# Second half of the modulation sums: from VectorE to ScalarE and GpSimd

## The chip, the cores and the metric

The kernel runs on one core of a Trainium2 chip. The core has TensorE (PE) for matrix products, VectorE (DVE) and ScalarE (ACT) for work on rows of elements, GpSimd (POOL) for the same without access to PSUM, and SyncE (SP), whose queue issues the loads here. The metric is device time in microseconds of one execution, as the median over runs.

## The reference

Two transformer blocks on 256 tokens of 1024 features, in float32. The first has a modulation vector, two attentions with gates, and a mixture of 32 experts of which each token takes 4; the second has three attentions, gates and a feed-forward part. What bears on the change is the modulation:

```
mod_x = (silu(c) @ w_ada + b_ada)[:, None, :]          # 1024 -> 6 x 1024
sh_a, sc_a, g_a, sh_m, sc_m, g_m = split(mod_x, 6)
...
x = x + g_a * merge(attention(modulate(rmsnorm(x), sh_a, sc_a)))
x = x + g_m * moe(modulate(rmsnorm(x), sh_m, sc_m))
```

The first two parts are needed before the first projection. The other four (`g_a`, `sh_m`, `sc_m`, `g_m`) are needed at the end of the attention and in the expert part.

## The kernel before, in words

The kernel goes through three stages: a dense one (projections of the first block, its two attentions, gates, output), the experts, and the second block. All weights pass through a ring of tiles of 128x2048 floats (1 MB each) that SP's queue loads in the order of a list, `specs`; a tile's slot is given back by `free(key)`, and the next load waits for a slot. Each weight of a dense projection is split into two parts that TensorE multiplies in turn: ACT copies it rounded (`wh`, L316), DVE subtracts (`wl`, L319). Split tiles rotate over a few buffers.

The first two parts of the modulation come from TensorE (`ada_first`). The other four come in two groups (g = 1 and 2) of 2048 columns each. For a group the list holds eight `ada` tiles (j = 0 to 7), 128 rows of `w_ada` each, spread among the weights of the projections. `ada_one`, called when certain weight quarters are done, takes the next such tile and multiplies it by the column `ada_s[:, j, 0:1]` (one value for each partition). For each half of 1024 columns it adds the product to an accumulator, `ga_b` (first half) or `gm_b` (second half), at L626; for j = 0 it writes the product alone, at L624. After j = 7 matmuls with a matrix of ones add the accumulators over the partitions (L633), and transposes bring the result into `mod` and `abp`.

Between the projections the kernel works through a list of small steps (`bg`), among them the attentions. `attend_a` has 16 units: scores on PE, their maximum on DVE (L831, L832), the exponential on ACT (L834), the reciprocal on DVE (L835), the scale of the probabilities on POOL (L856), transposes on PE (L866), copies on DVE or ACT, and the product with the values (L878). `attend_b` has 8 units of two maps each: the second map is scaled on POOL (L917), DVE combines it with the first (L918), then come transposes (L926), copies (L928) and products (L936).

The program is written in the order of the code, and a planner sets the order of each engine's instructions, with estimates of their durations and with semaphores for all dependencies; on the chip each engine runs its own list strictly in that order.

Of the kernel before, what the change touches and what calls it, by code (L numbers as in the profile page):

```python
# [13 lines left out]
AF = mybir.ActivationFunctionType  # L14
OP = mybir.AluOpType
# [3 lines left out]
D = 1024  # L19
# [56 lines left out]
def build(tc, I, out):  # L76
    nc = tc.nc
    V, S, G, PE = nc.vector, nc.scalar, nc.gpsimd, nc.tensor
# [12 lines left out]
    def bank(which="a", dt=F32, shape=(128, 512)):  # L91
        return psp.tile(list(shape), dt, name="bank_" + which, tag="bank")
# [172 lines left out]
    def free(key):  # L265
        live.pop(key)
        in_extra.discard(key)
        fill()
# [162 lines left out]
    gm_b = keep.tile([128, D], F32, name="gm_b")  # L431
# [84 lines left out]
    def body():  # L516
# [10 lines left out]
        ga_b = p1.tile([128, D], F32, name="ga_b")  # L527
# [31 lines left out]
        ada_s = p1.tile([128, 8, 32], F32, name="ada_s")  # L559
# [10 lines left out]
        for tt in range(2):  # L570
            scaled = G.tensor_scalar(out=xn[:, tt], in0=x_sb[:, tt], scalar1=rx[:, tt:tt + 1], scalar2=1.0,
                                     op0=OP.mult, op1=OP.mult)
# [43 lines left out]
        def ada_one():  # L616


            g, j = ada_queue.pop(0)
            w = live[("ada", g, j)]  # L620
            for c, acc in enumerate((ga_b, gm_b)):
                o = slice(1024 * c, 1024 * c + 1024)
                if j == 0:
                    V.tensor_scalar(out=acc, in0=w[:, o], scalar1=ada_s[:, j, 0:1], scalar2=None, op0=OP.mult)  # L624
                else:
                    V.scalar_tensor_tensor(out=acc, in0=w[:, o], scalar=ada_s[:, j, 0:1], in1=acc,  # L626
                                           op0=OP.mult, op1=OP.add)
            free(("ada", g, j))
            if j < 7:
                return  # L630
            ps = bank("b")
            for c in range(4):
                PE.matmul(ps[32 * c:32 * c + 32], one_row, (ga_b, gm_b)[c // 2][:, 512 * (c % 2):512 * (c % 2) + 512],  # L633
                          start=True, stop=True)
            mrow = p1.tile([128, 512], F32, name="mrow", tag="mrow")
            V.tensor_copy(mrow, ps)
            pt = bank("b", shape=(128, 4, 128))
            for i in range(4):
                PE.transpose(pt[:, i], mrow[:, 128 * i:128 * i + 128], ident)
            bias = cols[:, 48 + 16 * g:64 + 16 * g].rearrange("p (c i) -> p i c", c=4)  # L640
            V.tensor_tensor(mod[:, g], pt.rearrange("p i (c r) -> p i c r", r=32)[:, :, :, 0:2],
                            bias.unsqueeze(3).to_broadcast([128, 4, 4, 2]), op=OP.add)
            ps = bank("b", shape=(128, 2, 2, 128))
            for b in range(2):
                for e in range(2):
                    PE.transpose(ps[:, b, e], mrow[:, 256 * b + e:256 * b + 256:2], ident)
            v = ps.rearrange("p b e (c r) -> p c b e r", r=32)[:, (2, 0)[g - 1]:(4, 2)[g - 1], :, :, 0]
            for h in range(2):
                V.tensor_tensor(abp[:, 2 - g, h], v[:, h], cols_p[:, g - 1, h], op=OP.add)
            if g == 2:  # L650
                V.scalar_tensor_tensor(out=abp[:, 0], in0=abp[:, 0], scalar=1.0, in1=cols_p[:, 2], op0=OP.add,
                                       op1=OP.mult)
            if g == 1:
                grow = cg.rearrange("p k t d -> p (k t d)")
                add_row(grow, 0, mrow, 0)
                late["row"] = grow
            if g == 2:
                add_row(mrow, 2, mrow, 1)
                late["rows"] = mrow

        ada_step.append(ada_one)

        def add_row(dst, c0, mrow, k):
            brow = pp.tile([128, 512], F32, name="brow", tag="pexp1")
            for h in range(2):
                b0 = 32 * (c0 + h)
                f0 = 2048 + 3072 * k + 512 * h
                with tc.issue_after(split_last[0].ins):
                    nc.scalar.dma_start(out=brow[b0:b0 + 1], in_=I["b_ada"][:, f0:f0 + 512])
                V.tensor_tensor(dst[b0:b0 + 1], mrow[b0:b0 + 1], brow[b0:b0 + 1], op=OP.add)  # L670
# [314 lines left out]
        for tt in range(2):  # L985
            G.tensor_scalar(out=xc[:, tt], in0=xc[:, tt], scalar1=rc[:, tt:tt + 1], scalar2=1.0,
                            op0=OP.mult, op1=OP.mult)
# [74 lines left out]
        for k in range(2):  # L1062
            V.scalar_tensor_tensor(out=lj, in0=lams[:, 2 * k], scalar=1.0, in1=lams[:, 2 * k + 1],
                                   op0=OP.mult, op1=OP.mult, accum_out=lam[:, k:k + 1])
# [18 lines left out]
        while ada_queue:  # L1083
            ada_one()
# [27 lines left out]
        for h in range(2):  # L1112
# [3 lines left out]
            for q in range(4):  # L1116
# [5 lines left out]
                for m in range(4):  # L1122
                    for k in range(2):
                        i = 2 * (q % 2) + k
                        o = dst[m // 2][:, m % 2]
                        c = slice(128 * m, 128 * m + 128)
# [7 lines left out]
            for b in range(2):  # L1134
                j = 4 * h + 2 * b
# [8 lines left out]
                               op0=OP.add, op1=OP.mult)  # L1144
# [884 lines left out]
```

## Time and profile before

| | us |
|---|---|
| median of 3 runs | 1704.33 |
| lowest, highest | 1698.94, 1705.49 |
| profiled execution | 1698.37 |
| its span | 1696.6 |

In the profiled execution PE is busy for 1621.6 us of the span, DVE for 695.2, ACT for 466.0 and POOL for 81.8. Busy times are averages over stages with different limits, so they are read stage by stage: which engine or transfer has no gap there, and what the others wait for. A matmul's end is modelled, so a busy PE need not be PE at its peak. POOL's spans are rough.

### The profile page before, as it was taken

To read this page: it belongs to the slowest core of one execution; us is meant where nothing else is said; L and a number is where in the kernel's file an instruction comes from. 1 tells how busy PE (TensorE), PEld (TensorE's weight loads), DVE (VectorE), ACT (ScalarE), POOL (GpSimd) and SP (SyncE) were. 2 spreads that over 40 slices of the span, in tenths; PEclk is the share of its full clock that TensorE was granted. 3 is DMA by queue.
4 is the path that set the end of the run, shared out by engine and by line. 5 is a ranking of instruction groups with operands and counts; after the bars stand their busy time and mean duration, and the time that the engine had idled before them with its cause. 6 is when DMAs were issued, how large, how long until landed. Compare 5 with 4: busy or idle time off the path is not lost. (4 is left out here: it accounts for less than half of the span.)

```text
span 1696.6 us, 22129 instructions
## 1 busy us (share of the span) xinstructions
PE 1621.6 (96%) x9024; PEld 1012.3 (60%) x9024; DVE 695.2 (41%) x1348; ACT 466.0 (27%) x768; POOL 81.8 (5%) x112
## 2 busy tenths in 40 slices
PE   5999899999999999899999999999999999999997
PEld 3777797544434443354344334433388899989996
DVE  4898986311121111221211111111267556665555
ACT  3435564101000100110000001000256445454443
POOL 2102100000000000000000000000004101100001
PEclk9999999999999999999999999999999999999999
DMA  9643588999999999999999999999973433565540
GB/s 344 260 154 141 202 282 335 382 425 425 426 426 425 425 425 426 382 425 425 425 426 425 425 426 426 426 422 424 405 277 102 146 121 131 178 218 184 176 153 25
DMA packets 117035, 537.42 MB, mean 317 GB/s; under 512 B 11666, under 2 KB 13438, under 8 KB 66754
## 3 DMA queue, kind: packets, MB, share of 16 engines
q1 hardware_dynamic: 112144, 532.19, 78.4%
q10 hardware_dynamic: 4610, 3.52, 0.7%
q8 instruction: 72, 1.18, 0.3%
q0 software_dynamic: 176, 0.26, 0.1%
q14 instruction: 33, 0.27, 0.0%
HBM read 534.88 MB, written 1.05 MB: 316 GB/s over the span
## 5 line engine op out<-in xcount | busy, mean ns | idle before, releaser
L1381 PE MATMUL bank_a<-w,xg 128*64 128x512 f32 x2048 | 522.5, 599 | 2.2 <-DMA w<-in_w_up_dram 2.2
L1381 PEld LDWEIGHTS bank_a<-w,xg 128*64 128x64 f32 x2048 | 182.7, 137 | 280.9 <-issue 258.5
L319 DVE TENSOR_TENSOR wl<-w,wh 128x1024 fp32r<-128x1024 f32 (+1 forms) x193 | 236.2, 1228 | 153.0 <-ACT wh L316 145.1
L316 ACT ACTIVATE wh<-w 128x1024 fp32r<-128x1024 f32 (+1 forms) x193 | 202.1, 1049 | 220.1 <-PE bank_a L389 98.7
L1381 PE MATMUL bank_a<-w,at 128*64 128x512 f32 x960 | 228.4, 595 | 6.5 <-DVE e L1409 5.0
L390 PE MATMUL bank_a<-hi,wl 128*128 128x256 f32 x640 | 180.3, 283 | 1.0 <-DVE wl L319 1.0
L388 PE MATMUL bank_a<-hi,wh 128*128 128x256 f32 x616 | 176.3, 287 | 1.1 <-ACT hi L474 0.6
L389 PE MATMUL bank_a<-lo,wh 128*128 128x256 f32 x616 | 174.3, 283 | 0.2 <-DVE lo L475 0.2
L1381 PEld LDWEIGHTS bank_a<-w,at 128*64 128x64 f32 x960 | 83.5, 137 | 146.6 <-issue 102.9
L513 ACT ACTIVATE y<-bank_a,ws 128x512 fp32r<-128x512 f32 x32 | 22.0, 687 | 443.1 <-PE bank_a L1381 429.9
L390 PEld LDWEIGHTS bank_a<-hi,wl 128*128 128x128 f32 x640 | 122.3, 192 | 1.4 <-DVE wl L319 1.4
L388 PEld LDWEIGHTS bank_a<-hi,wh 128*128 128x128 f32 x616 | 117.8, 192 | 3.2 <-issue 0.9
L389 PEld LDWEIGHTS bank_a<-lo,wh 128*128 128x128 f32 x616 | 118.1, 192 | 0.9 <-DVE lo L475 0.6
L514 DVE SCALAR_TENSOR_TENSOR y<-bank_a,ws,y 128x512 fp32r<-128x512 f32 x32 | 24.0, 751 | 217.9 <-ACT y L513 216.2
L1409 DVE TENSOR_SCALAR e<-bank_a 128x512 f32<-128x512 f32 x32 | 22.1, 691 | 187.1 <-PE bank_a L1381 185.9
L1399 ACT ACTIVATE e<-gs 128x512 f32<-128x512 f32 x32 | 20.2, 630 | 236.7 <-DVE gs L1398 225.2
L1291 PEld LDWEIGHTS bank_a<-gr,x_sb 128*128 128x128 f32 x512 | 64.2, 196 | 23.0 <-issue 19.5
L1398 DVE TENSOR_SCALAR gs<-bank_a 128x512 f32<-128x512 f32 x32 | 22.0, 691 | 131.2 <-PE bank_a L1381 115.8
L1291 PE MATMUL bank_a<-gr,x_sb 128*128 128x128 f32 x512 | 69.3, 286 | 0.7 <-DVE gr L1274 0.7
L1296 DVE TENSOR_SCALAR xg<-bank_a,abp 128x128 f32<-128x128 f32 x64 | 21.9, 404 | 107.7 <-PE bank_a L1291 107.5
L1299 ACT ACTIVATE xg<-bank_a,abp 128x128 f32<-128x128 f32 x64 | 24.2, 455 | 121.8 <-PE bank_a L1291 121.7
L354 PE MATMUL bank_b<-wh,hh 128*128 128x512 f32 x128 | 49.9, 390 | 0.0
(453 smaller groups left out, 2198.4 us busy)
## 6 DMA issues: line engine op xcount, KB each, us to landing
w<-in_w_up_dram SPq DMA_DIRECT2D x144, 1024.0 KB
w<-in_w_down_dram SPq DMA_DIRECT2D x136, 1024.0 KB
w<-in_w_gate_dram SPq DMA_DIRECT2D x128, 1024.0 KB
w<-in_w_in_dram SPq DMA_DIRECT2D x45, 1024.0 KB
w<-in_w_ada_dram SPq DMA_DIRECT2D x16, 1024.0 KB
w<-in_w_ada_dram SPq DMA_DIRECT2D x16, 512.0 KB
w<-in_w_out_dram SPq DMA_DIRECT2D x8, 1024.0 KB
w<-in_w_down_dram SPq DMA_DIRECT2D x16, 512.0 KB
```

The source lines that it names most:

```text
L316: split_last[0] = S.activation(r32(wh[:, :n]), t[:, o:o + n], AF.Copy)
L319: V.tensor_tensor(r32(wl[:, :n]), t[:, o:o + n], wh[:, :n], op=OP.subtract)
L354: PE.matmul(o, r32(sh), r32(mh), start=first, stop=False)
L388: PE.matmul(o, r32(wh[:, k, c]), r32(hi[:, j]), start=j == 0 and m % 2 == 0, stop=False)
L389: PE.matmul(o, r32(wh[:, k, c]), r32(lo[:, j]), start=False, stop=False)
L390: PE.matmul(o, r32(wl[:, k, c]), r32(hi[:, j]), start=False, stop=j == 7 and m % 2 == 1)
L513: S.activation(r32(hi), src, AF.Copy, scale=scale)
L514: V.scalar_tensor_tensor(out=r32(lo), in0=src, scalar=scale, in1=hi, op0=OP.mult, op1=OP.subtract)
L1291: PE.matmul(ps[:, k], x_sb[:, tt, o:o + 255:2], d["gr"][:, tt].rearrange("p e s -> p (e s)"), start=tt == 0, stop=tt == 1)
L1299: S.activation(xg[:, j], ps[:, k], AF.Identity, bias=abp_[:, 1, j:j + 1], scale=abp_[:, 0, j:j + 1])
L1381: state["mm"] = PE.matmul(ps[h][64 * ab:64 * ab + 64], lhs(j, ab), w[ab][:, e, 512 * h:512 * h + 512], start=bias is None and j == 0, stop ...
L1409: V.tensor_scalar(out=u_, in0=ps[h], scalar1=7.0, scalar2=-7.0, op0=OP.min, op1=OP.max)
```

## The change

For the second half of the columns, ACT multiplies the half of the `ada` tile in place by the column, and POOL adds it to `gm_b`. For j = 0 ACT writes the product straight into `gm_b`. The first half, with `ga_b`, stays on DVE with the same instructions, and is issued behind the second. The tile is given back when both halves are done.

```
             w = live[("ada", g, j)]
-            for c, acc in enumerate((ga_b, gm_b)):
-                o = slice(1024 * c, 1024 * c + 1024)
-                if j == 0:
-                    V.tensor_scalar(out=acc, in0=w[:, o], scalar1=ada_s[:, j, 0:1], scalar2=None, op0=OP.mult)
-                else:
-                    V.scalar_tensor_tensor(out=acc, in0=w[:, o], scalar=ada_s[:, j, 0:1], in1=acc,
-                                           op0=OP.mult, op1=OP.add)
+            sj = ada_s[:, j, 0:1]
+            if j == 0:
+                S.activation(gm_b, w[:, D:], AF.Copy, scale=sj)
+                V.tensor_scalar(out=ga_b, in0=w[:, :D], scalar1=sj, scalar2=None, op0=OP.mult)
+            else:
+                S.activation(w[:, D:], w[:, D:], AF.Copy, scale=sj)
+                G.tensor_tensor(gm_b, gm_b, w[:, D:], op=OP.add)
+                V.scalar_tensor_tensor(out=ga_b, in0=w[:, :D], scalar=sj, in1=ga_b, op0=OP.mult, op1=OP.add)
             free(("ada", g, j))
```

## Rows read from the trace of the kernel before

**Rows 1.** The page's 40 equal slices of the span, busy share in tenths.
```profile
PE   5999899999999999899999999999999999999997
...
DVE  4898986311121111221211111111267556665555
```

**Rows 2.** Busy time by stretch: instructions, granted clock, DMA share, GB/s.
```profile
core 0: us, PE busy (x) PEld busy (x) DVE busy (x) ACT busy (x) POOL busy (x), PEclk, DMA share, GB/s
80.00:120.00 40.00, 40.00 (x190) 32.87 (x189) 38.65 (x84) 14.06 (x22) 0.00 (x0) 1.00 0.46 166
120.00:140.00 20.00, 17.80 (x121) 14.65 (x121) 19.59 (x38) 8.33 (x16) 3.85 (x4) 0.91 0.73 253
140.00:180.00 40.00, 38.34 (x337) 29.96 (x335) 33.29 (x74) 22.38 (x50) 10.02 (x13) 1.00 0.33 115
180.00:200.00 20.00, 16.85 (x132) 14.23 (x129) 18.15 (x37) 12.15 (x26) 4.24 (x5) 1.00 0.43 141
200.00:220.00 20.00, 15.98 (x123) 14.10 (x122) 18.23 (x32) 11.14 (x23) 4.07 (x3) 0.98 0.84 254
320.00:1240.00 920.00, 894.08 (x4014) 383.29 (x4012) 175.13 (x375) 93.56 (x174) 0.31 (x1) 0.99 1.01 422
1240.00:1697.00 457.00, 441.73 (x3095) 401.12 (x3094) 276.43 (x403) 224.65 (x341) 44.30 (x65) 0.99 0.43 150
```

**Rows 3.** Lines L626 and L624 alone: ns min/median/max, first and last start.
```profile
L626 DVE SCALAR_TENSOR_TENSOR gm_b<-w,ada_s,gm_b x14: 1266/1276/1708, 87.7 to 217.7; 128x1024 f32<-128x1024 f32 x14
...
L624 DVE TENSOR_SCALAR gm_b<-w,ada_s x2: 734/740/747, 51.3 to 166.2; 128x1024 f32<-128x1024 f32 x2
```

**Rows 4.** Groups of ACT's instructions, 0 to 300 us: busy, mean ns, idle before.
```profile
L316 ACT ACTIVATE wh<-w 128x1024 fp32r<-128x1024 f32 x48 | 50.7, 1059 | 59.4 <-PE bank_a L356 26.9 <-PE bank_a L389 15.9 <-DMA w<-in_w_in_dram 12.6
L834 ACT ACTIVATE pexp<-bank_b,mx,rsqb 128x512 f32<-128x512 f32 x16 | 12.4, 777 | 10.9 <-DVE mx L832 10.9
```

**Rows 5.** DVE in order of time: start, duration, idle before.
```profile
50.64 0.75 DVE L624 TENSOR_SCALAR ga_b<-w,ada_s 128x1024 f32<-128x1024 f32 x1 [3.57 <-DMA w<-in_w_ada_dram]
```

**Rows 6.** POOL lines alone: ns min/median/max, first and last start.
```profile
L498 POOL TENSOR_TENSOR clo<-fn_t,chi x8: 735/744/1108, 41.3 to 68.8; 128x256 fp32r<-128x256 f32 x8
...
L856 POOL TENSOR_SCALAR pexp<-pexp,mx x16: 691/692/1719, 126.1 to 167.5; 128x512 f32<-128x512 f32 x16
...
L917 POOL TENSOR_SCALAR pexp<-pexp,mx,lam x8: 765/768/1654, 179.5 to 214.7; 128x512 f32<-128x512 f32 x8
```

**Rows 7.** POOL in order of time, end of the kernel.
```profile
1688.61 1.26 POOL L1966 TENSOR_TENSOR x_sb<-x_sb,nf 128x512 f32<-128x512 f32 x1 [0.79 <-ACT sq L1965]
```

**Rows 8.** DVE in order of time, `attend_b`.
```profile
202.81 1.26 DVE L626 SCALAR_TENSOR_TENSOR ga_b<-w,ada_s,ga_b 128x1024 f32<-128x1024 f32 x1
```

**Rows 9.** POOL in order of time, `attend_b`.
```profile
203.07 1.65 POOL L917 TENSOR_SCALAR pexp<-pexp,mx,lam 128x512 f32<-128x512 f32 x1 [4.87 <-DVE mx L835]
```

**Rows 10.** DVE in order of time, end of the kernel.
```profile
1687.69 0.21 DVE L413 SCALAR_TENSOR_TENSOR rs_t<-rs_y,rs_m 128x1 f32<-128x1 f32 x1
...
1688.58 1.30 DVE L413 SCALAR_TENSOR_TENSOR rs_t<-rs_y,rs_m 128x1 f32<-128x1 f32 x1
```

**Rows 11.** Groups of DVE's instructions, 140 to 220 us, shapes apart.
```profile
L319 DVE TENSOR_TENSOR wl<-w,wh 128x1024 fp32r<-128x1024 f32 x10 | 12.1, 1214 | 0.0
L626 DVE SCALAR_TENSOR_TENSOR gm_b<-w,ada_s,gm_b 128x1024 f32<-128x1024 f32 x7 | 9.4, 1336 | 0.0
L626 DVE SCALAR_TENSOR_TENSOR ga_b<-w,ada_s,ga_b 128x1024 f32<-128x1024 f32 x7 | 9.3, 1322 | 0.0
L918 DVE SCALAR_TENSOR_TENSOR pexp<-pexp,mx 128x512 f32<-128x512 f32 x8 | 6.0, 751 | 3.6 <-POOL pexp L917 3.6
```

**Rows 12.** DVE in order of time, 180 to 184 us.
```profile
181.17 1.28 DVE L626 SCALAR_TENSOR_TENSOR gm_b<-w,ada_s,gm_b 128x1024 f32<-128x1024 f32 x1
```

**Rows 13.** SP's queue in order of time, 180 to 190 us.
```profile
182.48 0.38 SPq L132 DMA_DIRECT2D w<-in_w_in_dram  x1
```

**Rows 14.** ACT in order of time, 186 to 190 us.
```profile
188.17 1.06 ACT L316 ACTIVATE wh<-w 128x1024 fp32r<-128x1024 f32 x1 [0.43 <-DMA w<-in_w_in_dram]
```

**Rows 15.** PE in order of time, 187 to 192 us.
```profile
189.75 1.16 PE L936 MATMUL bank_b<-vb,at 128*128 128x128 f32 x8 [1.97 <-ACT at L928]
```

## The prediction

> **What bounds the kernel now.** I read the slices of the page first: TensorE (PE) shows a nine in nearly every one of the forty, VectorE (DVE) is at eight and nine only in the first six or so [rows 1]. A modelled busy PE is no proof, so the stretches come next. In 320 to 1240 us the DMA share is 1.01 at 422 GB/s: the expert weights arrive at the rate that the memory gives, and nothing that the change touches runs there. In 1240 to 1697 us PE is busy 441.73 of 457 us [rows 2]. The change works in the dense stage before both, so what it wins or loses must show there, and is handed on: the expert stage lives on slots and activations that the dense stage gives up, and the last stage on the expert stage's end. I pass it on one to one, though prefetch could swallow a little of either sign.
>
> Inside the dense stage the reader should see two halves. From 80 to 120 us PE is busy 40.00 of 40 us, and DVE 38.65: both are full, but PE is the one without a gap. From 120 to 220 us PE is busy 17.80 + 38.34 + 16.85 + 15.98 = 88.97 of 100 us, so it stands for 11.0 us, while DVE still works 19.59 + 33.29 + 18.15 + 18.23 = 89.3 us [rows 2]. That is attention mixed with gate projections: chains of small steps over PE, DVE, ScalarE (ACT) and GpSimd (POOL). The 11.0 us, and a little time at a granted clock below 1.00 (0.91 in 120 to 140 us), are all that relief of DVE there could bring.
>
> **What is removed.** DVE loses the second half of each `ada_one`: 14 sums of 1.28 us and two first products of 0.74 us [rows 3], in all 14 x 1.28 + 2 x 0.74 = 19.4 us. The first half (`ga_b`) stays where it was.
>
> **What ACT gets.** Sixteen products of 128x1024 from SBUF to SBUF. The nearest row is the split copy L316 of the same size, 1.06 us, and the nearest with operands from SBUF, as `sj` is one, the exponential L834 of 512 columns, 0.78 us [rows 4]. I take the first, so 17.0 us; twice the second, 1.55 us, is the upper bound, 25 us. ACT was busy 8.33 + 22.38 + 12.15 + 11.14 = 54.0 of the 100 us [rows 2], so there is room; the cost is what stands behind a product in ACT's queue: the exponentials, the copies of transposed probabilities, the copies L316. One product per 10.6 us (sixteen over some 170 us) is met by one instruction in ten, which then waits half of 1.06 us: for the 32 exponentials of the two attentions 32 x 0.1 x 0.53 = 1.7 us. A third of it I let reach PE: 0.6 us. The first product may stand in the queue before its weights have landed: DVE stood 3.57 us for them [rows 5]. DVE still has that wait, and ACT would get one like it, with the split copy of the next weights behind it; cover for it is two split quarters ahead, so I cost it at nothing, at 3.6 us if that cover is gone.
>
> **What POOL gets.** Fourteen adds of 128x1024 (the two first products go straight into `gm_b`). No row has that size. POOL's two-input row at 256 columns takes 0.744 us [rows 6], at 512 columns 1.26 us [rows 7]; the line through them gives 1.26 + 2 x 0.52 = 2.29 us. Call it 2.3, in all 32 us; 3.3 us each is the upper bound, where POOL has to wait for its turn (the L917 scale went from 0.768 to 1.654 us [rows 6]).
>
> The Trainium skill speaks against this move: "GPSIMD Engine Reference", Engine selection, sends a two-input elementwise add to VectorE and puts GpSimd at about half its speed. The rows agree, 2.3 us against 1.28, and by that rule alone the add costs more than it saves, unless POOL's idle time hides it.
>
> It doesn't hide all of it. At 202.81 us DVE starts a `ga_b` sum and at 203.07 POOL a scale L917, which takes 1.65 instead of 0.77 us: it ends 0.65 us behind DVE's sum [rows 6, 8, 9]. The other way round, DVE's tiny L413 takes 0.21 us alone and 1.30 us at 1688.58, beside POOL's add of 1.26 us that starts at 1688.61 [rows 7, 10]. So a DVE instruction with two inputs in SBUF and a POOL instruction take turns, whole instructions at a time. "Advanced Engine Details and Errata", VectorE Performance Modes, in the Trainium skill says the same of the second port.
>
> What that gives back: from 140 to 220 us the DVE work that stays and reads two SBUF inputs is L319 12.1, `ga_b` 9.3 and L918 6.0, in all 27.4 us, of 33.29 + 18.15 + 18.23 - 9.4 - 0.74 = 59.5 us of DVE work that stays [rows 2, 3, 11], or 46%. An add of 2.3 us therefore holds up about 2.3 x 0.46 = 1.06 us of DVE work. Bounds are 0 (every add beside work on PSUM) and 2.3. So DVE's true relief is 1.28 - 1.06 = 0.2 us a sum, 3 us over fourteen. A third reaches PE: -1.0 us.
>
> **What is queued behind the adds.** POOL also scales the probabilities: 16 times in L856 (0.692 us) and 8 times in L917 (0.768 us) [rows 6], and DVE's combination and PE's transposes wait for it. Fourteen adds fill 14 x 2.3 = 32 of the 130 us between the first and the last `gm_b` sum [rows 3], 25%. A scale that meets one waits half of it: 24 x 0.25 x 1.15 = 6.9 us. A third, by the same choice as above (PE has its own projection work between the chains), is +2.3 us; all of it would be +6.9, none 0.
>
> **The weights' slots.** An `ada` tile now comes free at the end of product and add. Today DVE's sum of 181.17 us ends at 182.45, and a weight load goes out at 182.48; ACT waits for that load until 188.17, copies the transposed probabilities behind it, and PE stands 1.97 us for that copy [rows 12 to 15]. Product and add take 1.06 + 2.3 = 3.4 us, but need not queue behind DVE's work, so the slot can come free earlier or later. I take half the stall as won, -1.0 us; bounds -2 (the whole stall won) and +4 (product and add are 2.1 us longer than a sum, at two such loads).
>
> **The sum.** -1.0 (DVE) - 1.0 (slot) + 2.3 (scales behind adds) + 0.6 (ACT) = +0.9 us, on a profiled execution of 1698.37 us (span 1696.6, 1.8 us around it): 1699.3 us. The runs shown are 1698.94, 1704.33 and 1705.49, so the profiled one lies at their low end; the mean of all four is 1701.8 us, and on it the forecast is 1702.7 us.
>
> **The rivals.**
> *DVE's relief counts in full* (faster). If most adds fall beside reductions and PSUM copies, the chains get 1.28 us shorter at each step, and the slots come free sooner. PE then wins most of its 11.0 us: 8 to 9 us, some 1693 us. For it: DVE is at 89% while PE stands. Against it: 46% of the DVE work left collides.
> *POOL becomes the attention's bottleneck* (slower). A scale waits for a whole add, which itself waited for DVE, and DVE's next two-input instruction waits for the scale: 24 scales with 0.6 us each at PE, +14 us, 1716 us. It decides from 0.6 us of PE time per add (14 x 0.6 = 8.4 us). For it: the turns in [rows 7 to 10], and that the instruction order was set with POOL nearly empty. Against it: POOL is busy 4.07 of 20 us [rows 2].
> *The slots come late* (slower within the bound): +4 us in place of -1, 1707 us.
> *A new order*. Instructions are put in order by a planner, so even equal work may be interleaved otherwise, by some 3 us either way. It widens the others and gets no chance of its own.
>
> **How the numbers follow.** Chances: the wash 0.62, full relief 0.13, POOL as bottleneck 0.17, late slots 0.08. About 0.5%, 8.5 us, is what a measurement of this kernel can tell from no change: below 1695.8 is faster, above 1712.9 slower. Full relief lands below in most cases, POOL's above; some of the wash goes out on either side. That gives 0.12 faster, 0.71 same, 0.17 slower. The predicted time is the wash's, 1702.7 us. The range reaches from 1694 (full relief, nearly) to 1715 us (POOL's case, nearly): 1 in 10 lies on either side.
>
> **What would show it.** Right: DVE's rows lose 19 us, ACT's gain 17 us in groups of 1.06 us, POOL's gain fourteen adds of 2.3 to 3.3 us; DVE's L319 and L918 show instructions stretched by 1 us or more; L917 has idle or longer spans in front; PE's busy time in 120 to 220 us stays within 4 us of 89. The prediction is wrong if PE's gaps there shrink below 5 us (full relief) or pass 20 us (POOL), or if the expert stage's start moves without them.

## The result, and the profile after

The change makes the kernel slower: 1726.22 us median (1722.33 to 1728.65) against 1704.36 us (1698.94 to 1705.49) for the kernel before, four runs each; the ratio of the means is 1.0132, with a 95% interval of 1.0104 to 1.0161. The forecast was 1702.7 us with a range of 1694 to 1715 us. The profiled execution after took 1722.33 us, its span 1720.6 us. In the new file the lines behind the diff stand one further down (L422 stays, L866 becomes L867, L917 becomes L918); in the kernels of the experiments some stand further down still.

The slices of the page, PE, DVE and POOL, to be read beside [rows 1]:

```profile
PE   6889799999999999899999999999999999999997
...
DVE  4796888421211121112111211111168546665555
...
POOL 2222510000000000000000000000004101000001
```

DVE's busy total is 700.0 us where 695.2 us stood before, although 19.4 us of sums were taken off it. POOL, which the page before shows at nothing above two ahead of the experts, has a five in the fifth slice (172 to 215 us). The same stretches as in [rows 2]:

```profile
80.00:120.00 40.00, 36.78 (x158) 29.36 (x158) 40.00 (x95) 16.39 (x24) 12.48 (x5) 0.96 0.38 136
120.00:140.00 20.00, 16.81 (x82) 12.81 (x80) 16.26 (x35) 7.12 (x13) 1.53 (x3) 0.91 0.53 174
140.00:180.00 40.00, 33.32 (x275) 25.38 (x274) 28.50 (x61) 22.80 (x45) 13.79 (x14) 0.98 0.30 109
180.00:200.00 20.00, 17.70 (x139) 15.53 (x140) 15.53 (x21) 9.15 (x15) 10.70 (x6) 0.86 0.52 172
200.00:220.00 20.00, 14.80 (x105) 12.51 (x104) 18.10 (x34) 12.36 (x25) 9.36 (x7) 0.91 0.57 199
```

In 80 to 120 us, where PE had no gap, it now has 3.2 us of gaps, DVE is at 40.00 of 40 us, and the granted clock is 0.96 in place of 1.00. In the stretches behind it DVE isn't fuller than before; the clock is lower in four of the five rows. The new instructions, minimum, median and maximum in ns, first and last start in us:

```profile
L626 ACT ACTIVATE w<-w,ada_s x14: 1135/1150/1157, 58.8 to 217.0; 128x1024 f32<-128x1024 f32 x14
...
L627 POOL TENSOR_TENSOR gm_b<-gm_b,w x14: 2360/2497/3423, 60.0 to 218.3; 128x1024 f32<-128x1024 f32 x14
```

So the sizes were close to the forecast. But a stretch between two fixed times holds other work once something ahead of it is late; work is better followed by when it starts. The first and the last score of `attend_a`, of `attend_b`, and the experts' first and last matmul:

```profile
L362 PE MATMUL bank_b<-ka,qq x32: 387/492/503, 133.3 to 174.9; 64*128 64x512 f32 x32
...
L362 PE MATMUL bank_b<-kb_t,qq x16: 386/496/621, 195.9 to 234.1; 64*128 64x512 f32 x16
...
L1382 PE MATMUL bank_a<-w,xg x2048: 589/592/1061, 325.4 to 1202.9; 128*64 128x512 f32 x187
```

Before, the three first starts were 120.9, 174.9 and 302.2 us. They are late by 12.4, 21.0 and 23.2 us, and the end by 24.0 us (span 1720.6 against 1696.6). `attend_a` itself takes as long as before (133.3 to 175.1 us for its score matmuls, 120.9 to 162.3 us before, 41.8 against 41.4 us). The loss thus arises in two places above all, ahead of `attend_a` and between the two attentions, and 5 us more inside `attend_b` (38.8 us of scores against 33.6), of which some 3 us come back before the experts.

**Ahead of `attend_a`.** POOL in order of time (start, duration, idle before), the first of the adds there:

```profile
79.94 2.40 POOL L627 TENSOR_TENSOR gm_b<-gm_b,w 128x1024 f32<-128x1024 f32 x1 [6.48 <-issue]
85.90 2.36 POOL L627 TENSOR_TENSOR gm_b<-gm_b,w 128x1024 f32<-128x1024 f32 x1 [3.56 <-ACT w L626]
92.38 2.39 POOL L627 TENSOR_TENSOR gm_b<-gm_b,w 128x1024 f32<-128x1024 f32 x1 [4.12 <-ACT w L626]
```

DVE in order of time in the same stretch:

```profile
79.77 0.17 DVE L421 TENSOR_TENSOR rs_t<-rs_y 128x16 f32<-128x16 f32 x1
79.85 0.28 DVE L721 TENSOR_REDUCE kss<-sq 128x2 f32<-128x128 f32 x1
80.05 2.33 DVE L422 TENSOR_TENSOR rs_t<-rs_t,rs_m 128x16 f32<-128x16 f32 x1
82.31 0.27 DVE L721 TENSOR_REDUCE kss<-sq 128x2 f32<-128x128 f32 x1
...
85.96 0.68 DVE L721 TENSOR_REDUCE qss<-sq 128x8 f32<-128x512 f32 x1
86.55 1.73 DVE L421 TENSOR_TENSOR rs_t<-rs_y 128x8 f32<-128x8 f32 x1
...
92.69 2.12 DVE L404 TENSOR_SCALAR rs_m<-qss 128x16 f32<-128x16 f32 x1
```

L421, L422 and L404 belong to the Newton steps of a reciprocal root: 0.16 us of work on 16 columns or fewer. The L422 that starts 0.11 us behind the add ends with it (80.05 + 2.33 = 82.38, the add 79.94 + 2.40 = 82.34). So does L421 with the second add (88.28 and 88.26), and L404, which has one tensor input, with the third (94.81 and 94.77). DVE starts nothing behind them meanwhile. Not every instruction is caught: the reduction L721 of 85.96 us starts inside the second add and takes its usual 0.68 us. By groups, 40 to 262 us (busy, mean ns), L422 before and then L422 and L421 after:

```profile
L422 DVE TENSOR_TENSOR rs_t<-rs_t,rs_m 128x16 f32<-128x16 f32 (+2 forms) x15 | 2.5, 168 | 0.1
```
```profile
L422 DVE TENSOR_TENSOR rs_t<-rs_t,rs_m 128x16 f32<-128x16 f32 (+2 forms) x15 | 8.8, 584 | 0.1
...
L421 DVE TENSOR_TENSOR rs_t<-rs_y 128x16 f32<-128x16 f32 (+2 forms) x15 | 4.1, 270 | 0.1
```

Before, L421 had a mean of 167 ns over the same 15 instructions. Each of the two adds on one partition, now L671, took 675 ns; after the change it takes 2624 ns.

**Between the attentions.** POOL, DVE and PE in order of time:

```profile
172.90 6.17 POOL L627 TENSOR_TENSOR gm_b<-gm_b,w 128x1024 f32<-128x1024 f32 x2 [1.71 <-ACT gm_b L623]
```
```profile
174.33 5.28 DVE L671 TENSOR_TENSOR cg<-mrow,brow 1x512 f32<-1x512 f32 x2
179.64 0.16 DVE L836 RECIPROCAL mx<-mx 128x1 f32<-128x1 f32 x1
179.72 0.67 DVE L870 COPY pt<-bank_b 128x512 f32<-128x512 f32 x1
```
```profile
180.45 1.97 PE L879 MATMUL bank_b<-pt,va_sb 128*64 128x128 f32 x14 [4.01 <-DVE pt L870]
```

Two adds run back to back on POOL. DVE's two L671 turn from 1.35 us into 5.28 us; the reciprocal L836 and the copy L870 stand behind them in DVE's list, and PE stands 4.01 us for that copy. What PE waited for in all, from 40 to 262 us (us, times, longest):

```profile
PE bank_b L771 <- DVE kr L763: 6.1, 2, 3.2
PE bank_b L937 <- ACT at L929: 4.3, 3, 2.2
PE bank_b L879 <- DVE pt L870: 4.0, 1, 4.0
...
PE bank_b L867 <- POOL pexp L857: 2.3, 2, 1.8
PE bank_a L356 <- POOL clo L498: 1.9, 2, 1.4
```

The wait for keys (L771) didn't exist before; L937 was 2.6 us, L867 2.0 us, L356 for POOL's L498 0.3 us. So most of what grew is a wait for DVE, or for what stands behind it. The exception is that L498: small sums, three of which queue on POOL behind the add that ends at 71.40 us, and PE waits 1.6 us more than before.

I call **held time** what a DVE instruction takes beyond the shortest one of the same operation, tiles and shape in any run, summed over those of 40 to 262 us that exceed it by over 0.3 us. Before it is 2.8 us (6 instructions), after 24.0 us (16 instructions).

### The profile page after: what moved, and what is told of

Its sections match the earlier page's. It is cut to its first block, busy times and chain, and to the rows that moved or that the text cites. A ratio compares the mean times of both kernels' runs of the same rounds, so it can differ in the third digit from the quotient of the medians.

```text
span 1720.6 us, 22160 instructions
## 1 busy us (share of the span) xinstructions
PE 1630.9 (95%) x9024; PEld 1016.1 (59%) x9024; DVE 700.0 (41%) x1332; ACT 481.6 (28%) x784; POOL 116.9 (7%) x126
```

## The experiments

The theory that the two traces suggested was that of turns (the first expectations call it port theory): a POOL add keeps DVE's instructions out for its whole length, and the held time is the loss. The rivals were the products on ACT, the planner's new order (PE's and DVE's lists differ in every variant), and scales queued behind the adds. The table has all the runs; the held time is that of each run's profile.

| run | POOL's added work | held, us | median, us | ratio to before, interval |
|---|---|---|---|---|
| the change | 14 x 2.50 us | 24.0 | 1726.22 | 1.0132, 1.0104 to 1.0161 |
| e1, adds on DVE | none | 1.6 | 1709.14 | 1.0049, 1.0031 to 1.0066 |
| e2b, idle adds | 14 x 2.42 us | 24.8 | 1723.17 | 1.0134, 1.0117 to 1.0151 |
| e6, group 1 only | 7 adds | 13.5 | 1711.38 | 1.0058, 1.0039 to 1.0076 |
| e7, group 2 only | 7 adds | 13.2 | 1714.18 | 1.0072, 1.0050 to 1.0094 |
| e8, short adds | 14 x 0.25 us | 1.5 | 1700.14 | 0.9985, 0.9971 to 1.0000 |
| e9, short products | 14 adds | 23.9 | 2289.92 | see there |
| e10, short both | 14 short adds | 1.5 | 1699.20 | 0.9986, 0.9976 to 0.9996 |
| e11, short idle adds | 14 short adds | 2.8 | 1701.24 | 0.9997, 0.9987 to 1.0007 |
| e12, half adds | 14 x 1.30 us | 11.1 | 1708.71 | 1.0047, 1.0032 to 1.0062 |
| e13, short adds on DVE | none | 1.9 | 1700.54 | 1.0001, 0.9985 to 1.0017 |
| e14, idle scales | 14 x 1.04 us | 9.5 | 1706.44 | 1.0025, 1.0008 to 1.0043 |
| e15, quarter adds | 56 x 0.74 us | 15.6 | 1717.12 | 1.0101, 1.0080 to 1.0123 |

**e1: the adds back on DVE, the products left on ACT.**
```
-                G.tensor_tensor(gm_b, gm_b, w[:, D:], op=OP.add)
+                V.tensor_tensor(gm_b, gm_b, w[:, D:], op=OP.add)
```


> As the changed kernel, but the fourteen adds run on VectorE (1.2 us each); the products stay on ScalarE. Port theory (each add on GpSimd holds VectorE's instructions with two SBUF inputs, 21 us in the changed kernel): no holds, VectorE's work as before, so 1700 to 1708 us and no VectorE instruction stretched by over 1 us. Rival, products and order (products in ScalarE's queue that wait for weights, and the planner's new order, cost the 22 us): 1715 to 1728 us, as in the changed kernel.

1709.14 us, so just outside what the turn theory said: 13 of the 22 us are gone and the held time with them, but 8.6 us stay. That could be the products or the order; e8 and e13 take it up.

**e2b: the kernel before with adds that nobody reads.** Both halves stay on DVE; an add on POOL reads the weights and writes a tile that nobody uses.
```
+            if j:
+                G.tensor_tensor(b3["b_up"], w[:96, :D], w[:96, D:], op=OP.add)
```


> The kernel before with all sums on VectorE, and beside them fourteen adds on GpSimd of 96 partitions x 1024 columns whose result nobody reads. Port theory: VectorE keeps its 19.4 us of sums and gets about 20 us of holds on top, so more than the changed kernel: 1725 to 1745 us. Rival, products and order: nothing on ScalarE, so 1704 us plus whatever an order costs, under 1712. Rival, scales queued behind adds on GpSimd: +7 us at most, 1711 us.

```profile
L622 POOL TENSOR_TENSOR b_up<-w x14: 2332/2417/3336, 58.2 to 223.2; 96x1024 bf16<-96x1024 f32 x14
```

1723.17 us, 1.8 us below the turn theory's range and far from the rivals'. With no work moved and none taken off DVE, the adds alone cost what the change costs. Nothing waits for these adds' results, so it is not latency of the sums.

**e6 and e7: the change for one group of eight tiles alone.** In the change all adds of group 1 run ahead of `attend_a` (60.0 to 117.5 us), those of group 2 from its end on (172.9 to 218.3 us).
```
+            if g == 2:      # e7: g == 1
+                ... both halves on DVE, as before
```


> The change for the first group of eight tiles alone; the second group stays on VectorE. Port theory: the first group's share of the loss, which the changed kernel shows by its first attention score (133.3 against 120.9 us, +12): 1712 to 1718 us. Rival, scales queued behind adds: the first group's adds end before the first scale, so 1704 us.

> The change for the second group of eight tiles alone. Port theory: the rest of the loss, +8 to +12 us, 1712 to 1716 us. Rival, scales queued behind adds: all of the loss, 1722 to 1728 us.

10.8 and 13.6 us over before (medians, 1700.54 there), together 24.4 where the whole change costs 22. e6 came out 0.6 us below its range, e7 within. Each group of seven adds carries about half of the loss, so it is not the work of one bad place.

**e8, e9, e10, e11: the same order with shorter instructions.** The planner's order is fixed first; then single instructions are cut from 1024 columns to 16, so that every engine's list stays the same, instruction for instruction. That separates the duration of the work from the order.
```
+                ADDS.append(G.tensor_tensor(gm_b, gm_b, w[:, D:], op=OP.add))
...
     with _tile.TileContext(nc) as tc:
         build(tc, aps, out)
+    shorten(nc, 16)
```
`shorten` replaces the access patterns of the instructions in `ADDS` by ones of 16 columns, with the same waits. e9 has ACT's products in the list, e10 both, e11 the idle adds of e2b.

> The changed kernel, instruction for instruction in the same order on every engine; only, after the order was fixed, each of POOL's 14 adds is cut from 1024 columns to the first 16, so 1008 columns of the modulation sum are left out. Turn theory (a POOL add keeps DVE's instructions out, and that is the loss): the 24 us of held DVE time go, and the time falls from 1726 to 1700 to 1710 us; what is left above 1700 is ACT's products and the order. Order rival (the planner's new order is the loss, the adds fit in it): 1718 to 1728 us.

> The changed kernel in its own order again, POOL's adds whole; ACT's 14 products w<-w are cut to 16 columns after the order was fixed, so 1008 columns of them are left out. Turn theory: 1718 to 1726 us, since the adds still hold DVE; at most 4 us come back. Product rival (ACT's queue and the later release of the weights' slots are half of the loss): 1708 to 1716 us.

> The changed kernel in its own order with both products and adds cut to 16 columns: DVE is relieved of 19.4 us and nothing is put in their place. Turn theory: the time falls to 1694 to 1704 us, so at or below the kernel before. Order rival: 1712 us or more, since the order alone is then left.

> The kernel before with the 14 added POOL adds that nobody reads, in the same order as the run with them whole (1723 us); after the order was fixed they are cut from 1024 columns to 16. Turn theory: 1699 to 1707 us. Order rival: 1716 to 1724 us, since the adds were only what moved the order.

e8, the adds alone and then the stretches:

```profile
L644 POOL TENSOR_TENSOR gm_b<-gm_b,w x14: 219/254/1274, 60.0 to 195.1; 128x16 f32<-128x16 f32 x14
```
```profile
80.00:120.00 40.00, 40.00 (x190) 32.81 (x188) 39.61 (x97) 17.78 (x26) 2.07 (x4) 1.00 0.47 163
120.00:140.00 20.00, 19.22 (x127) 14.27 (x126) 13.21 (x29) 12.56 (x22) 3.46 (x5) 1.00 0.63 230
140.00:180.00 40.00, 36.91 (x328) 29.54 (x329) 29.23 (x67) 23.66 (x45) 12.73 (x16) 1.00 0.45 157
180.00:200.00 20.00, 16.54 (x124) 13.60 (x124) 17.95 (x39) 15.06 (x32) 4.97 (x7) 1.00 0.50 165
200.00:220.00 20.00, 17.83 (x144) 16.14 (x143) 14.05 (x29) 11.62 (x26) 2.51 (x4) 1.00 0.85 237
```

1700.14 us: in the change's own order and with all of ACT's products, shorter adds alone bring back everything. PE is full again in 80 to 120 us, and the granted clock is 1.00 in all five stretches. e11 agrees: 1701.24 us in the order in which whole idle adds made 1723. So the order costs nothing that can be measured, and the products next to nothing. The columns left out change the values that go into the router, but not the work behind it: PE executes 9024 matmuls in e8, e10, e12 and e13 as before, and their experts, first matmul to last, take 877.8 to 880.8 us (879.2 before).

e9 can be compared in the dense stage alone: with the scale left out of most columns, `gm_b` comes out different, the router sends tokens elsewhere, and PE executes 438 instructions of the part for overfull experts that no other run has; they go with the 2290 us. In the dense stage nothing came back: the scores of `attend_a` start at 138.1 us (133.3 in the change), those of `attend_b` at 198.3 us (195.9), and 23.9 us are held; why `attend_a` starts even later, no run shows. The product rival falls.

e10 leaves out both, so DVE is relieved of 19.4 us and nothing stands in their place:

```profile
80.00:120.00 40.00, 40.00 (x192) 32.42 (x190) 39.43 (x94) 15.24 (x26) 2.14 (x3) 1.00 0.49 166
```

1699.20 us, 2.5 us below before by the medians, 0.7 to 4.1 us by the interval. That is all that taking these sums off DVE is worth in this order.

**e12: half the columns.** `shorten(nc, 512)` on the adds, else e8.

> The changed kernel in its own order on every engine; after the order was fixed each of POOL's 14 adds is cut from 1024 columns to the first 512, so half of each add is left out. Turn theory: an add is held and holds for about half as long (1.26 us instead of 2.4), the held DVE time falls from 24 to 10 to 13 us, and the time comes to 1707 to 1714 us, between 1700 (16 columns) and 1726. Rival (only adds longer than what DVE has queued for PE cost anything, or one unlucky collision does): within 3 us of one of the two ends.

```profile
L644 POOL TENSOR_TENSOR gm_b<-gm_b,w x14: 1280/1302/2330, 59.5 to 203.3; 128x512 f32<-128x512 f32 x14
```

1708.71 us, held 11.1 us, between the ends as the turn theory had it. Three points in one and the same order now: 1.5, 11.1 and 24.0 us held, ratios 0.9985, 1.0047, 1.0132.

**e13: e1 with DVE's adds cut to 16 columns**, in e1's order.

> The kernel with products on ACT and adds on DVE (1709 us), in its own order; after the order was fixed DVE's 14 adds are cut from 1024 columns to 16, so 1008 columns of the sum are left out. If the 8.6 us that this kernel lost are its order and ACT's products, they stay: 1705 to 1710 us. If DVE's own adds, placed late and all at once between the two attentions, are what PE waits for, the time falls to 1697 to 1702 us.

1700.54 us, so the 8.6 us of e1 were neither its order nor the products, but DVE's own adds where they now stand. In e1, DVE between the attentions and then POOL:

```profile
168.58 1.27 DVE L628 SCALAR_TENSOR_TENSOR ga_b<-w,ada_s,ga_b 128x1024 f32<-128x1024 f32 x1
169.76 0.15 DVE L836 RECIPROCAL mx<-mx 128x1 f32<-128x1 f32 x1
169.84 1.21 DVE L627 TENSOR_TENSOR gm_b<-gm_b,w 128x1024 f32<-128x1024 f32 x1
170.96 1.22 DVE L319 TENSOR_TENSOR wl<-w,wh 128x1024 fp32r<-128x1024 f32 x1
```
```profile
168.83 4.50 POOL L857 TENSOR_SCALAR pexp<-pexp,mx 128x512 f32<-128x512 f32 x2 [3.67 <-DVE mx L836]
```

POOL's two scales start at 168.83 us and take 4.50 us in place of 1.38; DVE goes from one instruction with two inputs in SBUF to the next meanwhile, with one short reciprocal between, and PE stands 3.1 us for the scale. In e13 the same two scales (L874, from 169.08 us) take 2.32 us. In e1 the waiting thus goes the other way, POOL behind DVE. That wait is 3.1 of e1's 8.6 us; what the rest is made of is not shown. (e13's profiled execution took 1706.26 us, the upper end of its runs.)

**e14: idle instructions with one input.** As e2b, with a scale in place of the add.
```
+                G.tensor_scalar(out=b3["b_up"], in0=w[:96, :D], scalar1=1.0, scalar2=1.0, op0=OP.mult, op1=OP.mult)
```


> The kernel before with 14 added POOL instructions that nobody needs, as in the run with idle adds (1723 us), but with one input in place of two: a scale of 96x1024 from SBUF to SBUF. Turn theory in its narrow form (two inputs of POOL take DVE's way to SBUF, one does not): 1699 to 1705 us. Turn theory in its wide form (any POOL instruction on SBUF takes turns with DVE): an instruction of about 1.4 us, so 10 to 16 us of held DVE time and 1709 to 1717 us.

```profile
L622 POOL TENSOR_SCALAR b_up<-w x14: 1038/1042/2109, 61.3 to 212.0; 96x1024 bf16<-96x1024 f32 x14
```

1706.44 us, between the two expectations. 9.5 us are held, just under the 10 to 16 of the wide form and far above the 2.8 of the kernel before, so instructions with one input hold DVE too; but each scale is only 1.04 us long and costs less (0.25%, in an order of its own).

**e15: each add as four of 256 columns.**
```
+                for q in range(4):
+                    qs = slice(256 * q, 256 * q + 256)
+                    G.tensor_tensor(gm_b[:, qs], gm_b[:, qs], w[:, D + 256 * q:D + 256 * q + 256], op=OP.add)
```


> The whole change, with each POOL add written as four of 256 columns. If the length of the single hold decides (DVE's short instruction waits at most 0.7 us, then slips in between), the held DVE time falls to 6 to 10 us and the time to 1704 to 1711 us. If the total of POOL's work decides, the time stays at 1718 to 1728 us.

```profile
79.15 2.91 POOL L629 TENSOR_TENSOR gm_b<-gm_b,w 128x256 f32<-128x256 f32 x4 [6.02 <-issue]
```
```profile
79.25 0.67 DVE L422 TENSOR_TENSOR rs_t<-rs_t,rs_m 128x16 f32<-128x16 f32 x1
79.84 0.27 DVE L723 TENSOR_REDUCE kss<-sq 128x2 f32<-128x128 f32 x1
80.04 0.57 DVE L423 SCALAR_TENSOR_TENSOR rs_y<-rs_t,rs_y 128x16 f32<-128x16 f32 x1
80.53 0.21 DVE L735 TENSOR_TENSOR t<-kr,sgn 128x64 f32<-128x64 f32 x1
80.67 0.71 DVE L421 TENSOR_TENSOR rs_t<-rs_y 128x16 f32<-128x16 f32 x1
```

1717.12 us, just below what the total would give, and far above what the single hold would. DVE slips one instruction in between two adds, and the next small one is held again: 0.67, 0.57, 0.71 us for 0.16 us of work. By the ratios splitting wins back a quarter of the loss (1.0101 against 1.0132), but the two intervals overlap, so even that isn't certain.

## Why the prediction was wrong

**The work removed, ACT and POOL: right in size.** ACT's products took 1.15 us (forecast 1.06, bound 1.55) and cost nothing measurable: e8 with whole products and e10 without differ by 0.9 us, where the sum had 0.6 us. The wait for weights that the sum put at nothing is there (ACT stands 12.8 us for `ada` tiles, 14.2 us in e8), and e8 loses nothing by it. POOL's adds took 2.36 to 3.42 us, forecast 2.3 to 3.3 us.

**The hold: mis-sized.** I took 46% of an add, 1.06 us, since 46% of DVE's busy time has two inputs in SBUF. Measured: (24.0 - 2.8) / 14 = 1.5 us for each add. The busy share is the wrong weight. DVE's list is strictly in order, and on it stand many short instructions of 0.15 to 0.3 us; while an add of 2.4 us runs, one that needs its turn comes up, in the twelve cases of the change, 0 to 1.6 us after the add's start (0.4 us in the median), and then waits for all the rest. So 21.2 us were held where 19.4 us were removed: the relief was -1.8 us, not +3 us. The kernel before gives a hint of that in [rows 10], where the 0.21 us of L413 became 1.30 us; I used it for the existence of turns and not for who is caught.

**"A third reaches PE": the step that failed.** I used one exchange rate for time taken off DVE and for time put on it. The removed sums were filler: all 19.4 us gone were worth 2.5 us (e10), an eighth. The held instructions stand ahead of what PE needs next (root, key rotation, transposes; reciprocal, copy, product), and their loss arrives in full. In the change's own order 24.0 - 1.5 = 22.5 us held cost 1.0132 / 0.9985, so 25 us; 11.1 - 1.5 = 9.6 us cost 1.0047 / 0.9985, so 10.6 us; for the idle adds 24.8 - 2.8 = 22.0 us cost 1.0134 / 0.9997, 23 us. (The ratio of the change is from another set of runs than the others.) That a little more than the held time is lost may be the lower granted clock behind PE's gaps and the 1.6 us for L498; no run separates them. With these figures relief and hold come to about -2.5 + 25 us, where the sum had -1.0 us for both together; 22 us were measured.

**The stretch from 80 to 120 us: read wrongly.** I set it aside because PE was the engine without a gap and looked for effects in 120 to 220 us alone. But DVE was at 38.65 of 40 us there with PE's key transposes next in line; behind five adds from 79.9 to 120 us PE waited 6.1 us for keys. Beside the two adds before them, from 60 us, PE's busy time fell by another 3.5 us (16.19 of the 20 us from 60 to 80, 19.70 before). In all 12.4 of the 24 us were lost before `attend_a` began. Of my own signs, PE's gaps in 120 to 220 us missed it: they went from 11.0 to 17.4 us, by [rows 2] and the rows after, not past 20. Two others saw it: PE's busy time there fell by 6.3 us, over the 4 us allowed, and the experts' start moved by 23.2 us, of which those gaps explain 6.4.

**Scales behind adds, +2.3 us: not seen.** PE waited 2.3 us for L867 where it had waited 2.0 us; the scales mostly came when no add ran. The rival "POOL becomes the attention's bottleneck", with 1716 us the nearest in time, thus isn't what happened: the attention's scales didn't queue on POOL; DVE's list was held by it.

**Slots, -1.0 us: wrong in mechanism, small in effect.** SP's queue waited for DVE's first half, now issued last, and hardly for POOL (2.2 us, once):

```profile
SPq L132 <- DVE ga_b L628: 70.2, 11, 16.0
SPq L132 <- DVE ga_b L624: 33.5, 1, 33.5
```

e8 keeps that order and that dependency and runs at 1700 us, so they cost nothing by themselves.

**Order and passing on: right.** A new order made no difference that can be measured (e8, e11), and the dense stage's loss reached the end one to one: 23.2 us at the experts' start, 24.0 us at the end.

**Is there a faster version?** e10 gives the bound for this order: with nearly all of the second half's work gone from every engine, 2.5 us were won, 4.1 us at the end of the interval. Whether another place for these sums wins more isn't shown.

## What to carry to other kernels

Before moving work off a busy engine, ask what the removed work was: filler in an in-order list can be worth a fraction of its time (here an eighth), while a wait put on a short instruction that others wait for can cost all of it, as here. Work given to an idle POOL isn't hidden when DVE is busy: weigh it by how soon DVE's next instruction with two inputs in SBUF comes up, not by DVE's busy share. To separate an order from the work in it, fix the order and shorten the work; to see the price of a helper engine alone, add its work to the old kernel without using the result.

## What the runs showed of the hardware that was not expected

- A POOL instruction on SBUF holds a DVE instruction with two inputs in SBUF however small it is: 16 columns of 0.16 us took 2.33 us, one partition of 512 columns (L671) 2.5 to 2.7 us in place of 0.68. L404, with a single tensor input of 16 columns, was held too and took 2.12 us. Others weren't stretched: the reduction L721 of 128x512 in SBUF (0.68 us inside an add), scales of one column, L833 (0.20 us each at 200.2 and 200.3 us, inside the add that ends at 201.3 us), and those that read PSUM. The maximum L832 kept a mean of 679 ns over 32 (682 before), the copy L870 of 685 ns over 8 (683 before).
- The Trainium skill, "SBUF — State Buffer", section "SBUF: two separate sides", says that DVE and GpSimd share a pair of ports that whoever starts first keeps for its whole instruction; of DVE's instructions it names those with two inputs in SBUF and those in a mode with two ports. The trace agrees to within 0.04 us (ends at 82.38 and 82.34 us), and e1 shows the other direction (POOL's scales took 4.50 us). Whether L404 with one tensor input runs in such a mode, no run here shows.
- One input instead of two makes POOL's instruction shorter (1.04 against 2.42 us for 96x1024), and the held time shrinks with it (9.5 us in e14 against 24.8 in e2b, 2.8 before), but it does hold.
